# A two-layer hybrid backbone: RWKV block inverses from 16-blocks, alternating array halves, reordered filter positions, four column groups for the conditioning products

## The chip, the core and the metric

The kernel runs on one core of one Trainium2 chip as one program. The metric is the device time of one execution in microseconds (us). TensorE (PE) multiplies, VectorE (DVE), ScalarE (ACT) and GpSimd (POOL) do the elementwise work, SyncE (SP) issues nearly all DMAs. The profile shows weight loads of TensorE apart (PEld). Every instruction queue works in order; the program is built by a tile framework whose scheduler simulates the engines and writes out one fixed order for each of them.

## The reference, cut to what matters

Layer 0 runs retention and RWKV-7 side by side, layer 1 a Hyena long convolution and a neighbourhood attention. The change touches three parts.

RWKV-7 is a recurrence over 1280 tokens (256 of context, 1024 of latents), in both directions d, for 8 heads of width 64:

```python
def step(s, inp):
    r_t, w_t, k_t, v_t, kk_t, a_t = inp
    sa = jnp.einsum('bhvk,bhk->bhv', s, -kk_t)
    s = s * w_t[:, :, None, :] + sa[..., None] * (kk_t * a_t)[:, :, None, :] + v_t[..., None] * k_t[:, :, None, :]
    return s, jnp.einsum('bhvk,bhk->bhv', s, r_t)
```

The Hyena filters are a small network of the position, `h = sin(f2 * (sin(f1 * (z @ w1 + b1)) @ w2 + b2)) @ w3`, times a decay window, and go through an FFT of 2048 points. The conditioning (scale, shift and gate of both layers) is the product of silu(c) and silu(c_ctx), two vectors of 1024, with the weights `ada_w` of 1024 x 3072 per layer.

## The kernel before, in words

`phase_a` computes the conditioning of layer 0 (`ada_quarter`, eight blocks of 256 columns), the norm, the dense projections of layer 0 and the retention. `phase_b` is RWKV. `hyena_kernels` (filters and their spectra) begins in the last steps of `phase_b` and shares the time with `phase_c`, which projects layer 0 out. Then come the projections of layer 1, attention and the long convolutions.

**RWKV.** The tokens are cut into ten groups g of 128 tokens, each two chunks t of 64. Within a chunk the recurrence is a triangular system of 64 x 64 for each head and direction; per group there are 16 of them for each direction (2 chunks, 8 heads), direction 0 on partitions 0 to 63 and direction 1 on 64 to 127. Three stages are pipelined by `step(k)`: `recur` of group k-2, `merge` of group k-1, `stage1` of group k, with that priority.

- `stage1` calls `half` four times (direction d, head pair hp). `half` makes the low-rank products (`lora`, two weights, K of 64 rows), tanh, a running sum, exponentials, the scaled operands AR and BK and the transposes BT. Then the score products `sc` (K of 64 rows, one half of the partitions for each head h) are masked on DVE into Ga (the triangular matrices) and Gr. The tiles UV are cleared in one half by a memset on POOL, and the other half is loaded.
- `inverse` cuts each 64 x 64 triangle into two diagonal blocks of 32, writes them to DRAM (tensor la) and reads them back so that each partition holds one block (tile AL). It starts from an identity (RR, loaded from DRAM), runs 31 steps of a substitution with two DVE instructions each (`tm` and `RR`, L950 and L952), and sends the result back over DRAM (lt) into TT.
- `merge` joins the two 32-blocks by three products in a row (t11p, xp, t21p), each copied out of PSUM in two halves, by ACT and by DVE.
- `recur` does, for each chunk, the chain: `rp` from the state SP, `rp` from Ga, copies to RH, `up` with TT, copies to UV, `sp` into the state, two DVE instructions on S, copies to SP. The output products with Gr and the store of y follow.

UV and RH are cleared in the half that a product doesn't need, so that `rp` from Ga and `up` run over all 128 rows.

**Filling work.** `step` of `phase_b` also lets run the blocks of `RwkvOut` (FIN sets its buffers) and the rest of the conditioning, 32 blocks of 128 columns (`ada_gate`, `ada_cols`). In `ada_block` 8 products of 128 rows by 2 columns add up in one PSUM tile.

**Filters.** `hyena_kernels` takes for each channel tile, order and pair of positions the columns 2q+j, 2q+j+8, ... of `hid` as weights (stride 8), with K of 64 rows for each direction of the filter, and masks with the window on DVE.

## Time and profile before

| | us |
|---|---|
| three runs: 2420.06, 2421.17, 2431.53; median | 2421.17 |
| profiled execution, its own time | 2423.35 |
| its span, first to last instruction | 2421.6 |
| PE busy / DVE busy / ACT busy / POOL busy | 2233.8 / 1212.0 / 930.4 / 792.3 |
| mean granted TensorE clock, of full speed | 0.939 |

Busy time of PE is modelled from pipelined matmuls, so a busy PE isn't PE at its peak. A matmul in float32 appears as two instructions. Groups of instructions give the busy time of all, the mean time of one, and the idle time before them with what ended it.

### The profile page before, as it was taken

The page shows a single profiled execution, that of the slowest core. Times are in us where ns is not written, and L with a number is a line of the kernel's source. Part 1 is how long each engine was busy: PE and PEld are TensorE (multiplying, and loading weights), DVE is VectorE, ACT ScalarE, POOL GpSimd, SP SyncE. Part 2 cuts the span into 40 slices and gives each one's busy share as a digit, 9 for nine tenths or more (in the row PEclk, how much of TensorE's full clock was granted, in tenths as well). Part 3 has the DMA queues.
Part 4 walks back from the last instruction along what each step waited for, and adds up shares of the span by engine and source line. Part 5 has one row for each costly group of instructions (what it writes and reads, how often), then busy time and mean ns, then how long its engine had stood idle before and what let it go on. Part 6 is the DMA issues. An engine that isn't in the chain of part 4 may idle for free. (4 is left out here: it accounts for less than half of the span.)

```text
span 2421.6 us, 44498 instructions
## 1 busy us (share of the span) xinstructions
PE 2233.8 (92%) x16928; PEld 1880.8 (78%) x16928; DVE 1212.0 (50%) x3075; ACT 930.4 (38%) x1996; POOL 792.3 (33%) x1040
## 2 busy tenths in 40 slices
PE   7999999999989788899788999999989999989997
PEld 3778877777856677677676789889968888878987
DVE  6301222234348688777786645620036666634438
ACT  4321134445345353344335533322124444434432
POOL 2313626453556244333224433521120110010133
PEclk9999999999988687789979899999989999989999
DMA  7323334544276444455545334343166562275453
GB/s 246 94 75 105 118 113 128 151 122 135 91 212 183 113 122 129 108 136 143 132 121 169 118 122 141 118 147 109 57 178 162 148 168 83 65 226 153 133 175 122
DMA packets 398367, 325.16 MB, mean 134 GB/s; under 512 B 135038, under 2 KB 337928, under 8 KB 397898
## 3 DMA queue, kind: packets, MB, share of 16 engines
q1 hardware_dynamic: 398154, 322.32, 46.2%
q8 instruction: 134, 2.20, 0.4%
q14 instruction: 79, 0.65, 0.1%
HBM read 227.06 MB, written 95.17 MB: 133 GB/s over the span
## 5 line engine op out<-in xcount | busy, mean ns | idle before, releaser
L380 POOL TENSOR_TENSOR wlo<-wraw,whi 128x512 fp32r<-128x512 f32 (+1 forms) x60 | 82.5, 1393 | 359.9 <-ACT whi L379 304.9
L412 PE MATMUL dps<-n1hi,whi 128*128 128x512 f32 x448 | 186.7, 417 | 0.1
L412 PE MATMUL dps<-n1hi,wlo 128*128 128x512 f32 x448 | 176.2, 393 | 0.0
L412 PE MATMUL dps<-n1lo,whi 128*128 128x512 f32 x448 | 176.0, 393 | 0.0
L412 PE MATMUL dnp<-wlo,nhi 128*128 128x512 f32 x400 | 159.8, 401 | 2.9 <-POOL wlo L396 2.9
L412 PE MATMUL dnp<-whi,nlo 128*128 128x512 f32 x400 | 158.6, 398 | 0.0
L412 PE MATMUL dnp<-whi,nhi 128*128 128x512 f32 x400 | 154.0, 401 | 1.3 <-ACT whi L395 1.3
L396 POOL TENSOR_TENSOR wlo<-wraw,whi 128x512 fp32r<-128x512 f32 (+1 forms) x72 | 92.3, 1291 | 134.8 <-ACT whi L395 124.9
L412 PE MATMUL mmps<-nhi,whi 128*128 128x512 f32 (+1 forms) x336 | 123.7, 369 | 2.4 <-ACT vto L527 2.3
L321 PE MATMUL adaps<-aw,sc 128*2 128x128 f32 (+1 forms) x640 | 112.9, 333 | 9.9 <-DMA aw<-in_ada_w 9.4
L412 PE MATMUL mmps<-nlo,whi 128*128 128x512 f32 (+1 forms) x336 | 120.9, 362 | 0.0
L412 PE MATMUL mmps<-nhi,wlo 128*128 128x512 f32 (+1 forms) x336 | 119.6, 365 | 0.0
L950 DVE TENSOR_TENSOR tm<-RR,AL 128x126 f32<-128x126 f32 (+22 forms) x310 | 99.7, 322 | 19.3 <-DMA AL<-la 11.9
L1248 POOL TENSOR_TENSOR hn<-hn,xr 128x256 f32<-128x256 f32 x60 | 47.2, 791 | 173.4 <-DVE hn L1247 157.4
L952 DVE TENSOR_TENSOR RR<-RR,tm 128x126 f32<-128x126 f32 (+22 forms) x310 | 97.1, 313 | 6.2
L412 PEld LDWEIGHTS dps<-n1hi,wlo 128*128 128x128 f32 x448 | 84.5, 189 | 18.5
L321 PEld LDWEIGHTS adaps<-aw,sc 128*2 128x2 f32 x640 | 54.9, 94 | 53.7 <-issue 15.2
L412 PE MATMUL ops<-whi,clo 128*128 128x256 f32 x320 | 90.6, 290 | 5.4 <-DVE clo L1181 5.4
L412 PEld LDWEIGHTS dps<-n1hi,whi 128*128 128x128 f32 x448 | 85.5, 191 | 10.9 <-ACT whi L379 0.6
L412 PEld LDWEIGHTS dps<-n1lo,whi 128*128 128x128 f32 x448 | 85.2, 190 | 10.3
L412 PEld LDWEIGHTS dnp<-wlo,nhi 128*128 128x128 f32 x400 | 76.0, 190 | 22.1 <-POOL wlo L396 4.8
L412 PE MATMUL ops<-wlo,chi 128*128 128x256 f32 x320 | 91.7, 288 | 0.0
(400 smaller groups left out, 6235.6 us busy)
## 6 DMA issues: line engine op xcount, KB each, us to landing
aw<-in_ada_w SPq DMA_DIRECT2D x32, 512.0 KB
kkr<-kkr SPq DMA_DIRECT2D x40, 384.0 KB
wraw<-in_odd_w_in SPq DMA_DIRECT2D x56, 256.0 KB
wraw<-in_even_w_in SPq DMA_DIRECT2D x48, 256.0 KB
bi<-in_nab SPq DMA_DIRECT2D x64, 192.0 KB
aw<-in_ada_w SPq DMA_DIRECT2D x8, 1024.0 KB
spec<-KS SPq DMA_DIRECT2D x32, 256.0 KB
h<-hn SPq DMA_DIRECT2D x16, 512.0 KB
```

Source lines behind the costliest of these rows:

```text
L321: nc.tensor.matmul(ps[0:2, :n], self.sc[:, k, :], w[:, k, :], start=k == 0, stop=k == 7)
L380: (lo_eng or nc.gpsimd).tensor_tensor(lo[:, kk:kk + 4], raw, hi[:, kk:kk + 4].bitcast(F32), op=ALU.subtract)
L396: nc.gpsimd.tensor_tensor(lo[:, :n], raw[:, :n], hi[:, :n].bitcast(F32), op=ALU.subtract)
L412: nc.tensor.matmul(ps, a, b, start=start and n == 0, stop=stop and n == 3 * nk - 1)
L950: nc.vector.tensor_tensor(t3, RR[:, 0:n, q:q + 1].to_broadcast([P, n, w]), AL[:, q:q + 1, q + 1:32].to_broadcast([P, n, w]), op=ALU.mult)
L952: nc.vector.tensor_tensor(RR[:, 0:n, q + 1:32], RR[:, 0:n, q + 1:32], t3, op=ALU.add)
L1248: add.tensor_tensor(h[:, cs], h[:, cs], x[:, cs], op=ALU.add)
```

## The change

- The inverse takes 16 x 16 diagonal blocks: 15 steps with two DVE instructions each. The block result RR is also transposed on POOL (RT), and both go over DRAM into full 64 x 64 tiles dd and dt. Their off-diagonal parts are zeroed in DRAM once. The DRAM tensors have a row pitch in which the diagonal blocks of all matrices stand 1040 elements apart.
- N is Ga without its diagonal blocks, masked on POOL. `merge` forms HT from N and dt, and then three times X = dd + (HT times X). Each of the four products comes in two halves of eight matrices, through one PSUM tile each, and X is added on DVE.
- `rp` from Ga and `up` use only the 64 rows that hold data; RH has one half as many columns. The memsets of UV, RH and TT are gone.
- Low-rank products of both directions are issued in turn (`lora`), score products of both heads in turn, `sp` with the head as the inner loop. PSUM has three tiles `b1` in place of two and one for lora.
- y is stored by a DMA on ACT's queue. FIN is 5 in place of 6.
- `ada_block`: the vectors stand in 32 columns (30 of them zero), and product k goes to column group k % 4; the four sums are added by a later product with a selection matrix `sel`. The gate blocks need one product more for it.
- Filter positions stand in the order in which they are used, so the weights are 128 columns in a row; both directions are one product of 128 rows by 256 columns with a zero-padded w3, and one DVE instruction masks them.

```diff
-        self.sc = sc
+        self.sc = self.cp.tile([P, 8, 32], F32, name="scw")
+        nc.gpsimd.memset(self.sc, 0.0)
+        nc.vector.tensor_copy(self.sc[:, :, 0:2], sc)
...
         for k in range(8):
-            nc.tensor.matmul(ps[0:2, :n], self.sc[:, k, :], w[:, k, :], start=k == 0, stop=k == 7)
-        return ps[0:2, :n]
+            g = 32 * (k % 4)
+            nc.tensor.matmul(ps[g:g + 32, :n], self.sc[:, k, :], w[:, k, :], start=k < 4, stop=k > 3)
+        return ps[:, :n]
...
+        for j, w in enumerate((self.w2, self.a2)):
+            for q in range(2):
+                p = 2 * hp + q
+                for d in range(2):
+                    nc.tensor.matmul(pss[d][:, j, q, :], w[HALF[d], p * P:(p + 1) * P], wa[HALF[d], j, :], start=True, stop=True)
...
-                for h in range(2):
-                    ps = b1([P, 4, P], "sc")
-                    for p in range(4):
-                        u = (p % 2) * NS + t
-                        nc.tensor.matmul(ps[:, p, :], bks[d, p // 2][HALF[h], u, :], R["ar"][d, p // 2][HALF[h], u, :],
+                pss = [b1([P, 4, P], "sc") for _ in range(2)]
+                for p in range(4):
+                    u = (p % 2) * NS + t
+                    for h in range(2):
+                        nc.tensor.matmul(pss[h][:, p, :], bks[d, p // 2][HALF[h], u, :], R["ar"][d, p // 2][HALF[h], u, :],
...
-                nc.gpsimd.memset(UV[HALF[d]], 0.0)
...
+        for d in range(2):
+            nc.sync.dma_start(mats(LA, d), gu[d])
+        AL = pi.tile([P, 16, 16], F32, name="AL", tag="AL", bufs=2)
+        nc.sync.dma_start(AL, blocks(LA))
+        for d in range(2):
+            nc.gpsimd.tensor_tensor(N[HALF[d]], gu[d], s.k("off")[HALF[d], None, :].to_broadcast([C, 16, C]), op=ALU.mult)
+        RR = pi.tile([P, 16, 16], F32, name="RR", tag="RR", bufs=2)
+        nc.gpsimd.tensor_copy(RR, self.eye)
+        tm = pi.tile([P, 64], F32, name="tm", tag="tm", bufs=2)
+        for q in range(15):
+            n, w = q + 1, 15 - q
...
+        RT = pi.tile([P, 16, 16], F32, name="RT", tag="RT", bufs=2)
+        nc.gpsimd.tensor_copy(RT, RR.rearrange("p s t -> p t s"))
+        for L, src, n in ((LD, RR, "dd"), (LT, RT, "dt")):
+            nc.sync.dma_start(blocks(L), src)
+            T = R[n] = pl.tile([P, 16, C], F32, name=n, tag=n, bufs=1)
+            for d in range(2):
+                nc.sync.dma_start(T[HALF[d]], mats(L, d))
...
+        for j in range(4):
+            new = HT if j == 0 else TT
+            for b in (0, 8):
+                ps = self.pc.tile([P, 8, C], F32, name="mg", tag="mg")
+                for u in range(8):
+                    for d in range(2):
+                        lh, rh = (N, Dt) if j == 0 else (HT, X)
+                        nc.tensor.matmul(ps[HALF[d], u, :], lh[HALF[d], b + u, :], rh[HALF[d], b + u, :], start=True, stop=True)
+                bs = slice(b, b + 8)
+                if j == 0:
+                    nc.scalar.copy(new[:, bs], ps)
+                else:
+                    nc.vector.tensor_tensor(new[:, bs], ps, Dd[:, bs], op=ALU.add)
...
-            for h, p, d in each:
+            for p, d, h in itertools.product(range(4), range(2), range(2)):
                 nc.tensor.matmul(sp[HALF[h], p, d, :], R["bt"][d, p // 2][:, (p % 2) * NS + t, h * C:h * C + C], uh(d, t, p, h),
...
-                    for j in range(2):
-                        nc.tensor.matmul(ps[:, j, :], hid[r, 2 * q + j::8], w3[r], start=True, stop=True)
-                    nc.vector.tensor_tensor(HK[:, hf], ps, win[:, hf], op=ALU.mult)
+                ps = psp.tile([P, 2, 2, P], F32, name="hkps", tag="mm")
+                for j in range(2):
+                    n2 = 2 * q + j
+                    nc.tensor.matmul(ps[:, j].rearrange("p h c -> p (h c)"), hid[:, n2 * P:n2 * P + P],
+                                     w3.rearrange("p h c -> p (h c)"), start=True, stop=True)
+                nc.vector.tensor_tensor(HK, ps.rearrange("p j h c -> p h j c"), win, op=ALU.mult)
```

On PE, at the merge of one group in the middle of `phase_b`, before (t11p, xp and t21p are the merge, lora and up belong to `half` and `recur`):

```order
L973 MATMUL t11p<-cst,TT_6116 32x32 x32
L851 MATMUL lora<-wa,a_6097 128x128 x2
L851 MATMUL lora<-wa,w_6096 128x128 x2
L973 MATMUL xp<-TX,Ga 32x32 x32
L851 MATMUL lora<-wa,a_6097 128x128 x2
L973 MATMUL t21p<-TT_6116,TY 32x32 x32
L851 MATMUL lora<-wa,w_6096 128x128 x2
L996 MATMUL up<-RH,TT_6116 64x64 x16
```

The same place on PE after the change (mg are the halves of the four merge products, btp the transposes, sc the score products):

```order
L1005 MATMUL mg<-dt,N 64x64 x16
L912 MATMUL btp<-cst,BK 128x128 x4
L944 MATMUL sc<-AR,BK 128x128 x8
L1005 MATMUL mg<-dd,HTt 64x64 x16
L944 MATMUL sc<-AR,BK 128x128 x12
L1005 MATMUL mg<-dd,HTt 64x64 x16
L944 MATMUL sc<-AR,BK 128x128 x12
L1005 MATMUL mg<-TT,HTt 64x64 x16
L858 MATMUL lora<-wa,w_6102 128x128 x2
L858 MATMUL lora<-wa,a_6103 128x128 x2
```

Three bursts of 32 products have become eight of 16, with other products of `stage1` between most of them.

On SP, the DMAs of one inverse and what stands between them, before (la and AL out and in, lt and TT the way back; the others belong to `stage1` and the conditioning):

```order
L940 DMA la<-Ga 32x16x32 x2
L954 DMA lt<-RR 1024x1x32 x2
L943 DMA AL<-la 64x1024
L841 DMA kkr<-kkr 128x6x128 x2
L943 DMA AL<-la 64x1024
L958 DMA TT_6116<-lt 32x16x32 x4
L945 DMA RR<-in_eyel 128x512
```

And after it (ld, lt, dd and dt are the way back):

```order
L970 DMA la<-Ga 64x16x64 x2
L331 DMA aw<-in_ada_w 128x8x128
L972 DMA AL<-la 128x16x16
L331 DMA aw<-in_ada_w 128x8x128
L908 DMA prod<-km 128x256
L878 DMA kkr<-kkr 128x6x128
L908 DMA prod<-km 128x256
L878 DMA kkr<-kkr 128x6x128
L987 DMA ld<-RR 128x16x16
L987 DMA lt<-RT 128x16x16
L990 DMA dt<-lt 64x16x64 x2
```

The way back has two stores and four loads in place of two and four, and the load of the identity is gone.

## Rows read from the trace of the kernel before

**Rows 1.** Busy time of each engine in stretches of the span, with the granted clock and the DMA share: the stretch of RWKV as a whole, its start, and parts of it.
```profile
core 0: us, PE busy (x) PEld busy (x) DVE busy (x) ACT busy (x) POOL busy (x), PEclk, DMA share, GB/s
690.00:740.00 50.00, 47.65 (x355) 32.42 (x351) 27.99 (x62) 33.16 (x81) 29.76 (x45) 0.93 0.78 208
760.00:1250.00 490.00, 411.81 (x5783) 355.26 (x5783) 388.10 (x1096) 198.63 (x460) 167.38 (x271) 0.82 0.51 129
800.00:850.00 50.00, 38.14 (x574) 33.51 (x573) 31.65 (x94) 17.98 (x43) 10.40 (x15) 0.70 0.39 90
1210.00:1220.00 10.00, 5.64 (x136) 5.36 (x136) 9.37 (x27) 1.80 (x4) 2.44 (x2) 0.50 0.22 72
1250.00:1440.00 190.00, 180.03 (x1243) 149.79 (x1236) 112.96 (x256) 92.45 (x186) 86.95 (x93) 0.91 0.42 137
```

**Rows 2.** Timeline (start, duration, instruction): the first substitution step of the first and the last of the ten inverses, the last store of an inverse, and the last burst of the merge that follows.
```profile
745.43 0.19 DVE L950 TENSOR_TENSOR tm<-RR,AL 128x31 f32<-128x31 f32 x1 [1.22 <-DMA AL<-la]
...
1206.02 0.19 DVE L950 TENSOR_TENSOR tm<-RR,AL 128x31 f32<-128x31 f32 x1 [6.89 <-DMA AL<-la]
...
1236.19 1.26 SPq L954 DMA_DIRECT2D lt<-RR  x2
...
1259.80 0.94 PE L973 MATMUL t21p<-TT,TY 32*32 32x32 f32 x28
```

**Rows 3.** Groups of the whole span: the two instructions of a substitution step (count, busy us, mean ns).
```profile
L950 DVE TENSOR_TENSOR tm<-RR,AL 128x126 f32<-128x126 f32 (+22 forms) x310 | 99.7, 322 | 19.3 <-DMA AL<-la 11.9
...
L952 DVE TENSOR_TENSOR RR<-RR,tm 128x126 f32<-128x126 f32 (+22 forms) x310 | 97.1, 313 | 6.2
```

**Rows 4.** Groups by shape in 760 to 1250 us: substitution steps of the sizes that remain, a DVE copy of the merge, a DVE addition from PSUM, two POOL instructions.
```profile
L950 DVE TENSOR_TENSOR tm<-RR,AL 128x16 f32<-128x16 f32 x10 | 2.2, 217 | 0.2
L950 DVE TENSOR_TENSOR tm<-RR,AL 128x45 f32<-128x45 f32 x10 | 2.1, 214 | 0.2
L952 DVE TENSOR_TENSOR RR<-RR,tm 128x45 f32<-128x45 f32 x10 | 2.4, 244 | 0.3
L950 DVE TENSOR_TENSOR tm<-RR,AL 128x70 f32<-128x70 f32 x10 | 2.7, 274 | 0.3
L975 DVE COPY TX<-t11p 32x512 f32<-32x512 f32 x10 | 6.9, 689 | 0.7 <-ACT TX L975 0.4
L1004 DVE TENSOR_TENSOR S<-S,sp 128x512 f32<-128x512 f32 x18 | 12.3, 686 | 12.1 <-PE sp L1002 11.7
L880 POOL TENSOR_TENSOR km<-km,kkr 128x256 f32<-128x256 f32 x33 | 26.7, 808 | 1.0
L925 POOL MEMSET UV<- 64x512 f32 x32 | 16.6, 518 | 116.0 <-PE sp L1002 84.9 <-PE rp L1010 28.9 <-ACT BT L887 2.1
```

**Rows 5.** Groups by shape in 760 to 1250 us: the products of RWKV and of the conditioning on PE.
```profile
L915 PE MATMUL sc<-AR,BK 64*128 64x128 f32 x544 | 73.4, 306 | 4.1 <-DVE Gr L919 3.9
L321 PE MATMUL adaps<-aw,sc 128*2 128x128 f32 x363 | 56.5, 313 | 0.5 <-DVE mc L289 0.5
L1002 PE MATMUL sp<-UV,BT 128*64 128x64 f32 x576 | 38.9, 242 | 3.6 <-DVE UV L999 3.6
L851 PE MATMUL lora<-wa,w 64*128 64x128 f32 x124 | 27.8, 355 | 0.7 <-ACT tw L855 0.7
L851 PE MATMUL lora<-wa,a 64*128 64x128 f32 x124 | 27.3, 352 | 9.1 <-ACT tw L855 9.1
L996 PE MATMUL up<-RH,TT 128*64 128x64 f32 x576 | 26.5, 261 | 11.5 <-DVE RH L993 7.8 <-DVE TT L975 3.6
L990 PE MATMUL rp<-UV,Ga 128*64 128x64 f32 x576 | 22.4, 228 | 0.0
L973 PE MATMUL t11p<-cst,TT 128*32 128x32 f32 x640 | 15.4, 206 | 7.5 <-DMA TT<-lt 7.5
L973 PE MATMUL xp<-TX,Ga 32*32 32x32 f32 x602 | 15.1, 215 | 5.2 <-DVE TX L975 5.2
L973 PE MATMUL t21p<-TT,TY 32*32 32x32 f32 x576 | 15.0, 221 | 8.8 <-DVE TY L975 8.7
```

**Rows 6.** Timeline: one burst of t21p, whose products alternate between two row tiles of 32 and write to one PSUM tile.
```profile
1083.98 1.20 PE L973 MATMUL t21p<-TT,TY 32*32 32x32 f32 x64
```

**Rows 7.** DMA in 1053 to 1056 us, nearly all packets of 128 bytes: count and MB, and the queue's share of 16 engines.
```profile
DMA packets 2061, 0.57 MB, mean 191 GB/s; under 512 B 1981, under 2 KB 1981, under 8 KB 2061
...
q1 hardware_dynamic: 2061, 0.57, 101.9%
```

**Rows 8.** Groups by shape in 1250 to 1600 us: filter products with their weight loads, and the mask on DVE.
```profile
L1320 PE MATMUL hkps<-hw,hid 64*128 64x128 f32 x256 | 61.2, 434 | 6.3 <-ACT S L1362 2.9 <-DVE HK L1321 2.1 <-DMA hw<-in_hw 0.6
L1320 PEld LDWEIGHTS hkps<-hw,hid 64*128 64x128 f32 x256 | 52.4, 326 | 16.1 <-ACT S L1362 4.6 <-issue 3.8 <-DVE HK L1321 3.1
```

**Rows 9.** The start: conditioning products of 256 columns in 0 to 150 us, one burst of them in the timeline, the last burst, and the DMA share in 40 slices of 0 to 50 us.
```profile
L321 PE MATMUL adaps<-aw,sc 128*2 128x256 f32 x128 | 32.5, 412 | 8.8 <-DMA aw<-in_ada_w 8.8
...
13.77 3.62 PE L321 MATMUL adaps<-aw,sc 128*2 128x256 f32 x16
...
50.70 3.62 PE L321 MATMUL adaps<-aw,sc 128*2 128x256 f32 x16
...
DMA  0689999999999999999999999999999996000000
```

**Rows 10.** Group in 690 to 760 us: conditioning products of 128 columns. And the wait of t21p for DVE in 800 to 1200 us (us in total, times, longest).
```profile
L321 PE MATMUL adaps<-aw,sc 128*2 128x128 f32 x151 | 24.3, 312 | 0.6 <-DMA aw<-in_ada_w 0.6
...
PE t21p L973 <- DVE TY L975: 7.3, 4, 3.6
```

More of the change, by code (lines that the diff above doesn't have):

```diff
@@ L34 @@
 SD = (8,)
-FIN = 6
+FIN = 5
 def _col(a):
@@ L334, in ada_gate @@
                 nc.sync.dma_start(ab[j:j + 1, :], src)
-            nc.vector.tensor_tensor(rows, ps, ab, op=ALU.add)
-            nc.sync.dma_start(gd[:, c0:c0 + n], rows)
+            nc.vector.tensor_copy(rows, ps)
+            ps = psp.tile([P, 512], F32, name="adag", tag="mm")
+            nc.tensor.matmul(ps[0:2, :n], self.sel, rows, start=True, stop=True)
+            nc.vector.tensor_tensor(ab, ps[0:2, :n], ab, op=ALU.add)
+            nc.sync.dma_start(gd[:, c0:c0 + n], ab)
             yield
@@ L900, in stage1 @@
             nc.sync.dma_start(wa[HALF[d]], D["wa"][HALF[d], :, t0:t0 + P])
+        for hp in range(2):
+            tws = self.lora(g, hp, wa)
+            for d in range(2):
+                R["ar"][d, hp], bks[d, hp], R["bt"][d, hp] = self.half(g, d, hp, tws[d], PCt)
         for d in range(2):
             ca, cr = (0, 64) if d == 0 else (64, 0)
-            for hp in range(2):
-                R["ar"][d, hp], bks[d, hp], R["bt"][d, hp] = self.half(g, d, hp, wa, PCt)
             m = s.k("m0") if d == 0 else s.k("m1")
@@ L941, in inverse @@
[L941 to L948 removed]
+        s, D, pi, pl = self.s, self.D, self.pi, self.pl
@@ new lines, in inverse @@
+        nc, C = s.nc, self.C
+        gu = [R["ga"][d].rearrange("p h t q c -> p (h t q) c")[HALF[d]] for d in range(2)]
+        N = R["n"] = pl.tile([P, 16, C], F32, name="N", tag="N", bufs=1)
+        mats = lambda t, d: t[d].rearrange("(u s t) -> s u t", s=65, t=C)[0:C]
+        blocks = lambda t: t.rearrange("d (a n) -> (d a) n", n=1040)[:, :1024].rearrange("a (s t) -> a s t", t=C)[:, :, 0:16]
+        LA, LD, LT = (D[n][g % 2] for n in ("la", "ld", "lt"))
+        for d in range(2):
+            nc.sync.dma_start(mats(LA, d), gu[d])
@@ L956, in inverse @@
[L956 to L975 removed]
+                                    AL[:, q:q + 1, q + 1:16].to_broadcast([P, n, w]), op=ALU.mult)
@@ new lines, in inverse @@
+            nc.vector.tensor_tensor(RR[:, 0:n, q + 1:16], RR[:, 0:n, q + 1:16], t3, op=ALU.add)
+        RT = pi.tile([P, 16, 16], F32, name="RT", tag="RT", bufs=2)
[3 more added lines that the diff above has]
+            T = R[n] = pl.tile([P, 16, C], F32, name=n, tag=n, bufs=1)
+            for d in range(2):
+                nc.sync.dma_start(T[HALF[d]], mats(L, d))
@@ new lines, in merge @@
+    def merge(self, R):
+        nc, pl, C, N, Dd, Dt = self.s.nc, self.pl, self.C, R["n"], R["dd"], R["dt"]
+        HT = pl.tile([P, 16, C], F32, name="HTt", tag="HT", bufs=1)
+        TT = R["tt"] = pl.tile([P, 16, C], F32, name="TT", tag="TT", bufs=2)
+        X = Dd
+        for j in range(4):
[3 more added lines that the diff above has]
+                for u in range(8):
+                    for d in range(2):
+                        lh, rh = (N, Dt) if j == 0 else (HT, X)
[5 more added lines that the diff above has]
+                    nc.vector.tensor_tensor(new[:, bs], ps, Dd[:, bs], op=ALU.add)
+            if j > 0:
+                X = TT
```

134 lines of the change are left out of this document (52 added, 82 removed).

## Prediction

> **What bounds the kernel now.** I read the table of stretches first, then the groups by shape inside the RWKV stretch, the timeline at its start and end, and the waits. PE is nearly full before and after RWKV; in RWKV it isn't. From 760 to 1250 us PE is busy 411.8 of 490 us at a mean granted clock of 0.82, DVE 388.1, the DMA engines 51%, POOL and ACT far less [rows 1]. So neither PE (84%) nor DVE (79%) fills the stretch; each waits in order for the other, and both are loaded enough that a microsecond taken from either shortens part of the period. The period is (1206.02 - 745.43) / 9 = 51.2 us from one inverse to the next [rows 2], so the stretch holds 490 / 51.2 = 9.57 groups, each with 43.0 us of PE and 40.6 us of DVE. The last inverse has no next group to hide behind: 30 us pass from its first step to its store, and its merge ends at 1260 us [rows 2], in a stretch where PE has 5.64 of 10 us and DVE 9.37 [rows 1]. From 1250 to 1440 us PE is busy 180 of 190 us [rows 1]: there filter products cost nearly what they take.
>
> **DVE in RWKV.** Before, 620 instructions take 99.7 + 97.1 us [rows 3], 19.7 us a group. After, 30 remain, on 15 to 64 elements a partition. The sizes from 16 to 70 took 214 to 274 ns [rows 4]; I take 235, so 7.05 us, which is 12.6 less. Against it, the merge's three DVE copies (0.69 us each) become six additions from PSUM, near 0.686 each [rows 4]: 2.0 more. DVE net: 10.6 less of 40.6.
>
> **PE in RWKV.** Busy time divided by count gives the cost of one instruction in a stream [rows 5]; two stand for a product.
> - Column halves: `sp`, eight products in a row into the same half, costs 38.9 / 576 = 67 ns; `rp` from Ga, which alternates, 22.4 / 576 = 39 ns. `sp` goes to 39: 64 x 28 ns = 1.8 us less.
> - Row halves: sc costs 135 ns and lora 222 ns, both with K of 64 rows. No row of before shows two 64-row tiles in turn; the nearest is t21p, two row tiles of 32 in turn, 1.20 us for 64, some 19 ns each [rows 6]. Bounds: no gain, or half the time. I take half, being nearer that row: 64 x 67 ns = 4.3 us and 32 x 111 ns = 3.6 us less.
> - Conditioning: 56.5 / 363 = 156 ns, 38 a group. Four column tiles in turn reach at best a quarter, 39 ns, which is also what Ga's products cost: 4.4 us less, at worst none.
> - Merge: 45.5 us / 9.57 = 4.75 us before; after, 128 products, 256 instructions. At 39 ns 10.0 us, so 5.2 more; at xp's 25 ns 1.7 more, at the 67 ns of `sp` 12.4 more.
> - `up` and Ga with half the rows: the same number of products and columns, so nothing.
>
> Net 8.9 us less of 43.0.
>
> The Trainium skill (TensorEngine Tiling (Array Packing), Restrictions and Gotchas, PSUM pressure) says that different row tiles cannot access the same PSUM bank at the same time. Here merge and `up` have both direction halves in one tile; sc and lora have one each. The burst of t21p alternates row tiles into one tile at 19 ns an instruction [rows 6], which doesn't look like a rule in force. By the rule merge would cost what `sp` does; that case is the second rival.
>
> **The rest of RWKV.** POOL loses two memset pairs a group (4 x 0.52 us) and gains two masks of 64 x 1024, two copies of 128 x 256 (0.81 us for the nearest row, so some 1.6; the masks at the same rate 3.2 each) [rows 4]: 17.5 us a group becomes about 23, which 45 us hide. If not, the transposed copy RT, alone in the chain, costs 0.8. DMA: the shapes give 2048 + 128 + 128 + 2048 + 2048 = 6,400 packets an inverse before, 2048 + 2048 + 4096 + 4096 = 12,288 after, of 64 and 256 bytes. A small packet held an engine for 1.019 x 3 us x 16 / 2061 = 24 ns [rows 7]; 5,888 more are 8.8 us on each of 16 engines. With 0.51 x 51.2 = 26 us now, that is 35 of 45 us: transfers get later, they don't become the bound. An inverse has a whole period of slack in the pipeline, except the last. y on ACT's queue frees SP; ACT has 199 of 490 us busy [rows 1], so I cost it at nothing, as FIN, whose blocks are filling work.
>
> **The period.** With PE lighter by 8.9 and DVE by 10.6 the period falls by less than PE's share, since the merge now makes eight trips PE, PSUM, DVE in place of three, all through one PSUM bank, and each trip is a wait in PE's queue unless other products stand between. I take two thirds, 6 us (bounds 2 and 10). Nine periods: -54 us (-18 to -90).
>
> **The end of RWKV.** 62 instructions took 30.2 us, 0.487 each with what stands between; 30 take 14.6, so -15.6. Late in its place: RT 0.8, the way back with 4,096 packets more (6.1 us at 24 ns over 16 engines), AL with 1,920 more (2.9). Net -6 (0 to -16).
>
> **Filters.** 256 instructions at 61.2 us, 239 ns, are near what their strided weight load takes, 52.4 / 256 = 205 ns [rows 8]. After, 128 instructions of 256 columns; the conditioning products of 256 columns cost 32.5 / 128 = 254 ns [rows 9], so 32.5 us: 29 less. PE is 95% busy there, but has waits of its own, so I take -24 (-10 to -32).
>
> **Start.** A burst of 16 takes 3.62 us, the last begins at 50.7 us, while the DMA engines are full until slice 34 of 40, 42 us [rows 9]. Four column groups make bursts near 0.9 us, then the weights' arrival bounds: at most 9 us, less what the modulation between bursts keeps. I take -7 (0 to -9).
>
> **Conditioning from 690 to 760 us.** 151 instructions, 24.3 us [rows 10], 161 ns; at 39 ns 18.4 less; the 16 selection products of the gates add 32 x 156 ns = 5. PE is 95% busy there [rows 1], but DVE's inverse starts too: half of 13.4, -7 (0 to -13).
>
> **Sum.** -54 - 6 - 24 - 7 - 7 = -98 us. Against the profiled execution's 2423.35 that is 2325; it stands 2.2 us above the median of 2421.17, so 2323. All ends together: -160 (2261) and -28 (2393).
>
> **Rivals.**
> 1. The clock takes it back. A lighter PE is granted a lower clock: 0.50 where it is busy 5.64 of 10 us, 0.70 in 800 to 850 us where it is busy 38.1 of 50 [rows 1]. If RWKV falls from 0.82 to 0.70, 34.1 us of PE become 40, the period falls by only 2: -18 - 6 - 24 - 7 - 7 = -62, 2359. Against it: DVE falls too, and what PE did before those stretches was wait.
> 2. Row tiles in one bank go one after the other: merge at 67 ns, +12.5 in place of +5.2, `up` +1.4. PE's balance is then nil, the period falls by 1 for DVE's sake, the last merge is 8 us longer: -9 + 2 - 24 - 7 - 7 = -45, 2376. The t21p burst speaks against it.
> 3. Slower: the merge's eight trips through one bank stall PE. Where t21p waited for DVE it was 7.3 / 4 = 1.8 us a time [rows 10]. Eight such are 14.4 us a group, of which some 2.2 are there today (7.5 + 5.2 + 8.8 us over 9.57 groups, [rows 5]): +12.2, so the period grows by 6.2: +56, the end +6, the others -38: +24, 2445. It decides from (98 + 22) / 80 = 1.5 us a trip. For it: one bank, and DVE works in order. Against it: the new order puts transposes, score or low-rank products between nearly all bursts.
>
> **Chances.** Forecast 0.58 (its own range 2261 to 2393), rival 1 0.15, rival 2 0.14, rival 3 0.10, and 0.03 for mixtures near no change. The range for 8 in 10 is 2258 to 2400: it holds the first three and leaves out rival 3 and a larger gain. A change under 0.5% (12 us) is about what a measurement here cannot tell from none. Faster: 0.58 + 0.15 + 0.14 = 0.87. Same: 0.03 and 0.01 of rival 3, 0.04. Slower: 0.09.
>
> **What would show it.** Inverses some 45 us apart; substitution steps near 235 ns and 300 in all; sc near 67 ns and lora near 111 by busy time over count, with their heads and directions in turn; merge near 39 ns, and its waits for DVE under 0.5 us a trip; filter products near 254 ns, 128 of them; the first dense product some 7 us earlier. A granted clock near 0.7 in RWKV speaks for rival 1, merge at 67 ns for rival 2, long PE waits for TT and HT for rival 3. The forecast is wrong if the period stays above 49 us, or if the gain is found mainly outside RWKV.

## The result, and the profile after

| | before | after |
|---|---|---|
| median of the runs beside each other, us | 2426.35 (4 runs) | 2457.15 (4 runs, 2451.81 to 2460.11) |
| ratio of after to before, 95% interval | | 1.0113 (1.0075 to 1.0151) |
| profiled execution, its own time / span | 2423.35 / 2421.6 | 2455.93 / 2454.1 |
| last dense product of layer 0 begins, us | 676.80 | 663.99 |
| first step of the first / the last inverse | 745.43 / 1206.02 | 744.26 / 1266.69 |
| period of the inverses | 51.2 | 58.0 |
| output projection of layer 0 begins | 1398.6 | 1425.2 |

The change made the kernel 1.1% slower; 4.1% faster was forecast. Nothing of the forecast gain of 6 us a period came: the period grew by 6.9 us, and nine of them are 62 us. From the last inverse to the output projection the change takes 158.5 us in place of 192.6, so that 27 of them are left where the projection begins, and 31 at the end.

The table of stretches, columns as in [rows 1], first the end of the first phase, then RWKV, then the filters:

```profile
690.00:740.00 50.00, 36.10 (x311) 25.07 (x311) 23.84 (x56) 26.36 (x62) 31.95 (x42) 0.74 0.72 206
760.00:1290.00 530.00, 400.29 (x6112) 354.80 (x6104) 338.67 (x823) 185.76 (x449) 209.64 (x279) 0.78 0.55 126
1250.00:1440.00 190.00, 150.65 (x1583) 125.40 (x1584) 119.39 (x268) 84.53 (x174) 76.03 (x78) 0.89 0.47 139
```

The reader is to see that both loaded engines are less loaded than before: PE 76% in RWKV (84% in [rows 1]), DVE 64% (79%). A group takes longer although no engine is full: the stretch is bound by who waits for whom.

The timeline answering to [rows 2]: the first step of the first and of the last inverse, its two stores (ld is the way back of RR, lt that of the transposed block), the last burst of the last merge.

```profile
744.26 0.17 DVE L981 TENSOR_TENSOR tm<-RR,AL 128x15 f32<-128x15 f32 x1 [0.79 <-DMA AL<-la]
...
1266.69 0.83 DVE L981 TENSOR_TENSOR tm<-RR,AL 128x15 f32<-128x15 f32 x1 [0.60 <-DMA AL<-la]
...
1279.10 0.37 SPq L987 DMA_DIRECT2D ld<-RR  x1
1279.77 0.71 SPq L987 DMA_DIRECT2D lt<-RT  x1
...
1335.52 1.10 PE L1005 MATMUL mg<-TT,HTt 64*64 64x64 f32 x32
```

Groups of the whole span, answering to [rows 3] and [rows 4]: the substitution, the merge's additions, the mask of N.

```profile
L974 POOL TENSOR_TENSOR N<-Ga,cst 64x1024 f32<-64x1024 f32 x20 | 47.0, 2351 | 162.0 <-DVE Ga L947 143.1 <-PE mg L1005 18.8
L981 DVE TENSOR_TENSOR tm<-RR,AL 128x15 f32<-128x15 f32 (+4 forms) x150 | 45.0, 300 | 24.0 <-DMA AL<-la 20.4
L983 DVE TENSOR_TENSOR RR<-RR,tm 128x15 f32<-128x15 f32 (+4 forms) x150 | 42.6, 284 | 3.3
L1010 DVE TENSOR_TENSOR TT<-mg,dd 128x512 f32<-128x512 f32 x60 | 41.1, 685 | 7.2 <-PE mg L1005 6.3
```

Groups by shape in 760 to 1290 us, answering to [rows 5]:

```profile
L944 PE MATMUL sc<-AR,BK 64*128 64x128 f32 x576 | 58.9, 311 | 0.0
L1005 PE MATMUL mg<-TT,HTt 64*64 64x64 f32 x1152 | 53.6, 260 | 30.9 <-DVE TT L1010 30.8
...
L1024 PE MATMUL rp<-SP,AR 128*128 128x128 f32 x256 | 44.6, 341 | 18.0 <-ACT SP L1046 15.2 <-ACT Yg L1053 2.7
...
L1005 PE MATMUL mg<-dt,N 64*64 64x64 f32 x578 | 29.7, 255 | 10.9 <-DMA dt<-lt 10.8
L1040 PE MATMUL sp<-UV,BT 128*64 128x64 f32 x544 | 27.8, 263 | 4.5 <-DVE UV L1037 4.5
L1034 PE MATMUL up<-RH,TT 64*64 64x64 f32 x544 | 26.7, 255 | 23.7 <-DVE TT L1010 23.7
...
L1005 PE MATMUL mg<-dd,HTt 64*64 64x64 f32 x576 | 22.2, 231 | 7.1 <-ACT HTt L1008 5.0 <-DVE TT L1010 2.1
L335 PE MATMUL adaps<-aw,scw 128*32 128x128 f32 x328 | 19.9, 339 | 14.8 <-DVE adab L352 6.4 <-DVE fv L1108 6.1 <-DVE mc L302 1.7
L858 PE MATMUL lora<-wa,w 64*128 64x128 f32 x128 | 18.4, 347 | 0.0
L858 PE MATMUL lora<-wa,a 64*128 64x128 f32 x128 | 16.5, 314 | 0.0
```

Busy time over count: sc 102 ns (135 before), lora 34.9 / 256 = 136 (222), sp 51 (67), adaps 61 (156), merge 105.5 / 2306 = 46. So the cheaper products are there. The waits before mg and up for TT, 30.8 and 23.7 us, catch the eye; e2 and e12 below speak against their setting the period.

Where the low-rank products stand in PE's order, with the engines whose signal they wait for (one group of the change; lora makes the first pair of a group after the score products, the second pair after two btp):

```
2836 L944 MATMUL sc<-AR,BK 128x128 [waits PE_49]
2837 L858 MATMUL lora<-wa,w_6102 128x128 [waits DVE_49,PE_49] x2
...
2849 L912 MATMUL btp<-cst,BK 128x128 [waits Pool_49]
2850 L912 MATMUL btp<-cst,BK 128x128 x3
2851 L858 MATMUL lora<-wa,w_6102 128x128 [waits Activation_49] x2
```

Per group, 4 low-rank tiles, 4 of transposes and 8 of scores take turns in three tiles b1, in the order of the program. The first pair therefore waits for DVE, which masks the scores of the group before, the second for ACT, which copies the transposes of the first head pair out; those in turn wait for POOL's BK, the end of the chain that begins with the low-rank products. Before the change the low-rank tile was apart and waited only for ACT's own tanh. In the trace (1101.76 btp, 1102.35 lora; 1129.73 to 1131.44 sc, 1132.75 lora):

```profile
1101.76 0.66 PE L912 MATMUL btp<-cst,BK 128*128 128x128 f32 x4
1102.35 0.71 PE L858 MATMUL lora<-wa,w 64*128 64x128 f32 x8
...
1129.73 1.71 PE L944 MATMUL sc<-AR,BK 64*128 64x128 f32 x19
...
1132.75 0.71 PE L858 MATMUL lora<-wa,w 64*128 64x128 f32 x8
```

And POOL in between, which makes BK, stands still behind the mask of N, whose Ga comes with those scores:

```profile
1115.56 0.73 POOL L907 TENSOR_TENSOR km<-km,kkr 128x256 f32<-128x256 f32 x1
1128.14 2.35 POOL L974 TENSOR_TENSOR N<-Ga,cst 64x1024 f32<-64x1024 f32 x1 [11.85 <-DVE Ga L947]
1132.26 2.36 POOL L974 TENSOR_TENSOR N<-Ga,cst 64x1024 f32<-64x1024 f32 x1 [1.77 <-DVE Ga L947]
1137.31 0.72 POOL L905 TENSOR_TENSOR km<-km,kkr 128x256 f32<-128x256 f32 x1 [2.70 <-issue]
```

The Trainium skill (Perfetto Trace Analysis, Optimization Strategy) says that the same gap repeating on the engine that should be saturated can mean that there isn't enough SBUF or PSUM for the next tile. POOL isn't such an engine here, but its gap of 11.85 us repeats: 137.8 us in 14 such waits for Ga between 800 and 1260 us. The trace agrees so far as the gap changes with the tiles: in e6 below, which shares out the PSUM tiles in another way, the same mask waits 82.7 us in 7 waits between 800 and 1200 us, and not for Ga but for merge, which still reads the one buffer of N.

Last, the stores of the eight output blocks (RwkvOut) at the end of RWKV, before and after (count, ns min/median/max, start of the first and the last), and the stores of y in 1150 to 1380 us, before and after:

```profile
L1096 SPq DMA_DIRECT2D cat<-fo x8: 370/370/1276, 1205.4 to 1397.4; - x8
```
```profile
L1134 SPq DMA_DIRECT2D cat<-fo x8: 370/371/371, 1206.5 to 1424.0; - x8
```
```profile
L1018 SPq DMA_DIRECT2D y<-Yg x14: 446/462/547, 1160.9 to 1291.4; - x14
```
```profile
L1056 ACTq DMA_DIRECT2D y<-Yg x16: 452/452/478, 1159.9 to 1364.2; - x16
```

The projection begins at 1398.6 and 1425.2, 1.2 us behind the last block's store in both. I call this row of blocks the train. In the change it started on time and took 217 us in place of 192. By the program its blocks come in pairs, each behind the y of a later group, and the last y is stored at 1364.2 in place of 1291.4. The fifth block shows such a wait: its first load of y (fa) is issued at 1303.0, its second (fb) only at 1320.6, behind a y stored at 1317.4; before the change the two are issued at 1285.5 and 1286.0, and the y of that group was there by 1245.9.

### The profile page after: what moved, and what is told of

It reads as the page before. It is cut to its first block, busy times and chain, and to the rows that moved or that the text cites. A ratio compares the mean times of both kernels' runs of the same rounds, so it can differ in the third digit from the quotient of the medians.

```text
span 2454.1 us, 45258 instructions
## 1 busy us (share of the span) xinstructions
PE 2174.1 (89%) x17472; PEld 1851.5 (75%) x17472; DVE 1155.3 (47%) x2771; ACT 918.7 (37%) x1986; POOL 825.7 (34%) x1039
## 5 line engine op out<-in xcount | busy, mean ns | idle before, releaser
L397 POOL TENSOR_TENSOR wlo<-wraw,whi 128x512 fp32r<-128x512 f32 (+1 forms) x60 | 81.7, 1380 | 353.4 <-ACT whi L396 274.3
L413 POOL TENSOR_TENSOR wlo<-wraw,whi 128x512 fp32r<-128x512 f32 (+1 forms) x72 | 92.2, 1290 | 119.8 <-ACT whi L412 114.8
L974 POOL TENSOR_TENSOR N<-Ga,cst 64x1024 f32<-64x1024 f32 x20 | 47.0, 2351 | 162.0 <-DVE Ga L947 143.1
L429 PE MATMUL ops<-whi,chi 128*128 128x256 f32 x320 | 92.3, 291 | 0.0
L429 PEld LDWEIGHTS dnp<-whi,nlo 128*128 128x128 f32 x400 | 75.2, 188 | 17.5 <-issue 1.7
L1005 PE MATMUL mg<-TT,HTt 64*64 64x64 f32 x1280 | 59.0, 259 | 32.8 <-DVE TT L1010 32.7
```

The source lines that it names most:

```text
L397: (lo_eng or nc.gpsimd).tensor_tensor(lo[:, kk:kk + 4], raw, hi[:, kk:kk + 4].bitcast(F32), op=ALU.subtract)
L413: nc.gpsimd.tensor_tensor(lo[:, :n], raw[:, :n], hi[:, :n].bitcast(F32), op=ALU.subtract)
L429: nc.tensor.matmul(ps, a, b, start=start and n == 0, stop=stop and n == 3 * nk - 1)
L974: nc.gpsimd.tensor_tensor(N[HALF[d]], gu[d], s.k("off")[HALF[d], None, :].to_broadcast([C, 16, C]), op=ALU.mult)
L1005: nc.tensor.matmul(ps[HALF[d], u, :], lh[HALF[d], b + u, :], rh[HALF[d], b + u, :], start=True, stop=True)
```

## Experiments

All runs on one table; the ratio is to runs of the kernel before on the same chip. Period: (first step of the last inverse - that of the first) / 9. Train: stores of the first and the last of the eight blocks, us.

| run | median | ratio (95%) | period | train |
|---|---|---|---|---|
| after | 2457.2 | 1.0113 (1.0075 to 1.0151) | 58.0 | 1207 to 1424 |
| e1 outer parts only | 2405.5 | 0.9904 (0.9873 to 0.9935) | 53.5 | 1204 to 1390 |
| e2 32-blocks in the change | 2477.3 | 1.0192 (1.0150 to 1.0234) | 60.2 | 1223 to 1449 |
| e3 merge shares b1 | 2656.5 | 1.0924 (1.0875 to 1.0973) | 84.3 | 1334 to 1630 |
| e4 mask on DVE | 2442.4 | 1.0035 (1.0011 to 1.0060) | 56.5 | 1226 to 1434 |
| e5 own low-rank tile | 2480.1 | 1.0200 (1.0152 to 1.0247) | 52.9 | 1308 to 1489 |
| e6 own tile and order | 2437.1 | 1.0011 (0.9983 to 1.0038) | 50.0 | 1252 to 1432 |
| e7 before, shared | 2585.3 | 1.0628 (1.0588 to 1.0667) | 64.3 | 1268 to 1491 |
| e8 = e6, mask on DVE | 2410.6 | 0.9918 (0.9890 to 0.9946) | 51.0 | 1215 to 1407 |
| e9 order alone | 2480.6 | 1.0206 (1.0157 to 1.0254) | 56.5 | 1305 to 1485 |
| e10 = e8, sc in turn undone | 2421.3 | 0.9960 (0.9934 to 0.9986) | 50.0 | 1237 to 1416 |
| e11 = e1, recurrence changed | 2427.3 | 0.9985 (0.9957 to 1.0013) | 52.1 | 1260 to 1427 |
| e12 longer merge | 2506.5 | 1.0310 (1.0263 to 1.0357) | 59.0 | 1313 to 1497 |
| e13 = after, blocks first | 2471.3 | 1.0161 (1.0134 to 1.0187) | 60.2 | 1259 to 1452 |
| e14 = e6, blocks first | 2403.2 | 0.9876 (0.9850 to 0.9901) | 50.4 | 1212 to 1392 |
| e15 = e8, blocks first | 2417.2 | 0.9937 (0.9913 to 0.9960) | 49.8 | 1236 to 1416 |
| e16 = e1, blocks first | 2418.5 | 0.9933 (0.9905 to 0.9962) | 52.9 | 1203 to 1388 |
| e17 before, longer blocks | 2443.8 | 1.0041 (1.0021 to 1.0062) | 50.8 | 1202 to 1431 |
| e18 after, longer blocks | 2486.4 | 1.0228 (1.0211 to 1.0246) | 57.6 | 1270 to 1476 |

Each edit makes the scheduler write a new order of everything. A difference under 15 us between two kernels can come from another order as well as from the edit; I draw conclusions from larger ones, or from periods.

**e1, outer parts only.** The class `Rwkv` of before with its tensors la and lt, all else of the change:

```diff
-FIN = 5
+FIN = 6
...
-    def lora(self, g, hp, wa):
...
+    def half(self, g, d, hp, wa, PCt):
```

> RWKV is left as it was; only the conditioning products on four column groups and the filter part are taken from the change. Theory (the whole loss sits in RWKV, the other parts gain): about 2426 - 13 (end of the first phase) - 15 (filters) = 2398, period between inverses 51 us. Rival (the outer parts cost something inside RWKV, since the conditioning blocks run there with more copies on DVE): 2420 or more, with a period above 52 us.

Measured 2405.5, ratio 0.9904: 26 us faster than the runs beside it. The outer parts gain and RWKV loses it. But the period is 53.5, not 51.2:

```profile
739.00:1220.00 481.00, 402.59 (x5341) 353.66 (x5340) 365.76 (x1023) 195.04 (x456) 173.31 (x286) 0.73 0.50 127
```

PE's busy time is 402.59 / 481 x 53.5 = 44.8 us a group at a clock of 0.73, 43.0 at 0.82 before, although conditioning products cost 69 ns in place of 156. Inside RWKV their gain isn't to be seen: the score products, which e1 leaves as they were, went from 135 to 82.3 / 543 = 152 ns (760 to 1200 us).

**e2, the inverse and merge of before in the change.**

```diff
-        for q in range(15):
+        for q in range(31):
...
-        for j in range(4):
+        for nm, rows, dst, op in (
+                ("t11p", e, lambda d: TX[e[d]], lambda d, u: (TT[:, u, 0:32], ident[:, e[d]])),
...
```

> The change with the inverse and the merge of before (32-blocks, 31 steps, three products); the alternating halves, the half-width products, no clearing, the new order of the low-rank and score products, the filters and the conditioning stay. Theory (the 16-block inverse with its long merge sets the period): the period falls from 58 to 47 to 51 us, 2350 to 2395. Rival (the new order of the low-rank and score products delays the triangular matrices): the period stays at 55 or more, 2430 to 2460.

Measured 2477.3, period 60.2. My theory of that time, that the long merge sets the period, fell: without the new inverse the change is 20 us slower still. The first step and the last:

```profile
745.35 0.19 DVE L978 TENSOR_TENSOR tm<-RR,AL 128x31 f32<-128x31 f32 x1 [4.35 <-DMA AL<-la]
...
1287.49 0.19 DVE L978 TENSOR_TENSOR tm<-RR,AL 128x31 f32<-128x31 f32 x1 [1.16 <-DMA AL<-la]
```

**e3, a second bank for merge, out of the b1 rotation.**

```diff
-                ps = self.pc.tile([P, 8, C], F32, name="mg", tag="mg")
+                if b and not last:
+                    ps = self.b1([P, 8, C], "mg")
+                else:
+                    ps = self.pc.tile([P, 8, C], F32, name="mg", tag="mg")
```

> The second half of each merge product goes to another PSUM tile (one of the three b1 tiles) for all groups but the last, so that a burst need not wait until DVE has emptied the tile of the burst before. Rival 3 of the prediction (one PSUM bank): the waits of merge for DVE fall from 31 us to under 10 and the time by 20 to 40 us, 2415 to 2435. Theory (the chain of dependent bursts, not the bank): within 10 us of 2457.

Measured 2656.5, period 84.3: neither. The question of the bank wasn't answered, since the tile came from b1; but it showed how much hangs on that rotation.

**e4, the mask of N on DVE.**

```diff
-            nc.gpsimd.tensor_tensor(N[HALF[d]], gu[d], s.k("off")[HALF[d], None, :].to_broadcast([C, 16, C]), op=ALU.mult)
+            nc.vector.tensor_tensor(N[HALF[d]], gu[d], s.k("off")[HALF[d], None, :].to_broadcast([C, 16, C]), op=ALU.mult)
```

> The mask that makes N is issued on DVE in place of POOL, so POOL no longer stands 138 us in the stretch behind the score products. Theory that POOL's order sets the period (the next group's scaled operands wait behind N): the time falls by 30 us or more, to 2425 or less. Theory (merge chain): the time stays within 10 us of 2457, since the merge is no earlier.

Measured 2442.4: 15 us less than the change, period 56.5. Between the two expectations, and no more than the 15 us above: POOL's order may cost something, the bulk lies elsewhere.

**e5 and e6, the low-rank tile apart, then the order too.** In e5 the products of one direction follow those of the other:

```diff
-        return self.pb.tile(shape, F32, name=name, tag="b1", bufs=3)
+        return self.pb.tile(shape, F32, name=name, tag="b1", bufs=2)
...
+        ps = self.pb.tile([P, 2, 2, P], F32, name="lora", tag="lo", bufs=1)
```

e6 on top of it:

```diff
-        for hp in range(2):
-            for d in range(2):
-                R["ar"][d, hp], bks[d, hp], R["bt"][d, hp] = self.half(g, d, hp, wa, PCt)
         for d in range(2):
+            for hp in range(2):
+                R["ar"][d, hp], bks[d, hp], R["bt"][d, hp] = self.half(g, d, hp, wa, PCt)
```

> The low-rank products go back to a PSUM tile of their own (one, as before), for one direction after the other; b1 has two tiles again; the order of the four calls of half, all else of the change and its inverse stay. Theory (shared rotation: the low-rank products of the next half wait until the transposes of this one are out, since they take turns in the same three tiles, so the halves no longer overlap): the period falls from 58 to 50 or less, 2345 to 2390. Rival (the order: score products only after all four halves): the period stays within 2 us of 58, 2440 to 2460.

> As the run before, and the score products of a direction again follow its two halves, as before the change; the score products of both heads still alternate. Shared rotation: no better than the run before by more than 10 us. Order: 20 us or more better than it.

The period falls from 58.0 to 52.9 and to 50.0; the times are 2480 and 2437. So the theory was right on the period, in the larger part, and wrong on the time: e5 has a period 5 us shorter than the change and is 23 us slower. Its first inverse begins 20 us later (764.7), its last still 25 us earlier (1241.2), but its train starts 101 us later. Of the 43 us from e5 to e6 (20 or more were expected of the order) nine periods of 2.9 us are 26; the train starts 55 us earlier. The first step of the first and the last inverse of e6:

```profile
743.90 0.15 DVE L970 TENSOR_TENSOR tm<-RR,AL 128x15 f32<-128x15 f32 x1
...
1194.05 1.76 DVE L970 TENSOR_TENSOR tm<-RR,AL 128x15 f32<-128x15 f32 x1 [2.36 <-DMA AL<-la]
```

The stretch of e6, and from its timeline what stands still in the train (POOL, then PE and DVE):

```profile
744.00:1194.00 450.00, 369.13 (x5711) 326.15 (x5711) 297.20 (x734) 187.15 (x441) 201.33 (x276) 0.82 0.62 140
```
```profile
1175.14 1.26 POOL L1114 TENSOR_TENSOR fa<-fa,lnwb 128x512 f32<-128x512 f32 x1 [4.29 <-DVE fa L1111]
```
```profile
1239.92 1.05 PE L1096 MATMUL bon<-rkh,fp 128*128 128x2 f32 x8
1241.01 0.69 DVE L1097 TENSOR_TENSOR fv<-fv,bon 128x512 f32<-128x512 f32 x1 [0.28 <-PE bon L1096]
1241.78 1.27 POOL L1098 TENSOR_TENSOR fv<-fv,lnwb 128x512 f32<-128x512 f32 x1 [31.18 <-DVE fv L1097]
```

The first block's sum fa is ready at 1176.4, its product bon, a filler in PE's order, comes at 1239.9.

**e7, the shared rotation in the kernel before.**

```diff
-        ps = self.pb.tile([P, 2, 2, P], F32, name="lora", tag="lo", bufs=1)
+        ps = self.b1([P, 2, 2, P], "lora")
...
-        return self.pb.tile(shape, F32, name=name, tag="b1", bufs=2)
+        return self.pb.tile(shape, F32, name=name, tag="b1", bufs=3)
```

> The kernel before with one edit: its low-rank tile takes its turn in the b1 rotation, of three tiles in place of two (as many banks in all). Shared rotation: it slows by 30 to 80 us, to 2455 to 2505, period 55 to 60. Rival (only the paired products or the order cost): within 10 us of 2426.

Measured 2585.3, 152 us slower (30 to 80 expected) with as many banks and no other edit; period 64.3:

```profile
767.66 0.19 DVE L950 TENSOR_TENSOR tm<-RR,AL 128x31 f32<-128x31 f32 x1 [2.88 <-DMA AL<-la]
...
1346.38 0.19 DVE L950 TENSOR_TENSOR tm<-RR,AL 128x31 f32<-128x31 f32 x1 [2.62 <-DMA AL<-la]
```

The longest waits of the stretch are those of the chain from the low-rank products to the transposes:

```profile
POOL AR L870 <- ACT Pt L864: 195.8, 28, 14.4
ACT BT L887 <- PE btp L885: 64.8, 24, 7.2
...
PE btp L885 <- POOL BK L879: 60.5, 18, 9.0
```

This is the plainest of the runs: the shared rotation by itself costs 13 us a period, more than the change loses. The change has it in a milder form; that this comes from its asking for low-rank tiles in pairs is likely, but no run shows it.

**e8, e6 with the edit of e4 on top** (the mask on DVE).

> Own low-rank tile and order as before, and the mask of N on DVE. Theory (once the halves overlap, POOL's wait behind the score products is what holds them next, as the 15 us of the run with the mask on DVE alone suggest): 5 to 20 us below the same kernel with the mask on POOL. Rival (the merge chain holds it): no difference over 5 us.

Measured 2410.6, 26 us less than e6, more than expected; the period is no shorter (51.0), the train starts 38 us earlier. The expected mechanism isn't what gained.

**e9, order alone.** Low-rank products of all four halves first, d the outer loop, three shared tiles.

```diff
-        for hp in range(2):
-            tws = self.lora(g, hp, wa)
-            for d in range(2):
-                R["ar"][d, hp], bks[d, hp], R["bt"][d, hp] = self.half(g, d, hp, tws[d], PCt)
+        tws = [self.lora(g, hp, wa) for hp in range(2)]
         for d in range(2):
...
+            for hp in range(2):
+                R["ar"][d, hp], bks[d, hp], R["bt"][d, hp] = self.half(g, d, hp, tws[hp][d], PCt)
```

> The change with one thing of its first stage undone in another way: the three shared tiles stay, but the low-rank products of all four halves come first, and the score products of a direction follow its two halves. The low-rank products of the second head pair no longer stand behind the transposes of the first. (Tiles for their results: 5 in place of 3; operands kkr: 2 in place of 3, as before the change.) Theory (low-rank products behind transposes and late score products are the loss, not the number of tiles): period 50 to 54, 2400 to 2440. Rival (any sharing of the tiles costs as much as in the kernel before with a shared rotation): 2480 or more, period 60 or more.

Measured 2480.6, period 56.5: the theory's 50 to 54 was missed. Even asked for early, low-rank tiles in the shared rotation hold the period; order alone is worth 1.5 us.

**e10, e8 with the score products of one head after the other; e11, e1 with the recurrence of the change** (half-width products, no clearing, sp in turn, y on ACT's queue). First e10's core, then two of e11's lines:

```diff
-                pss = [b1([P, 4, P], "sc") for _ in range(2)]
+                for h in range(2):
+                    ps = b1([P, 4, P], "sc")
```
```diff
-                nc.gpsimd.memset(UV[HALF[d]], 0.0)
...
-                nc.sync.dma_start(o[t if d == 0 else 1 - t], Y[r])
+                nc.scalar.dma_start(o[t if d == 0 else 1 - t], Y[r])
```

> The fastest version so far with the change's inverse (own low-rank tile, order as before, mask on DVE), its score products again one head after the other. Theory (pairs take both b1 tiles at once, so that products and masks take turns): 5 to 20 us faster, 2390 to 2405. Rival (alternating halves save PE time that counts): slower by 5 to 15 us.

> The outer parts of the change (run e1) and of RWKV only the recurrence: half-width products, no clearing of UV and RH, alternating state products, y stored from ACT's queue. Inverse, merge and first stage as before. Theory (what is alone on the loop gains, and POOL no longer waits 95 us for sp): 2375 to 2398. Rival (the stores on ACT's queue or half-width products cost): 2406 or more.

Both theories missed, both rivals came: e10 is 11 us slower than e8, which is within the 15 us above, e11 22 us slower than e1. In e10 sc costs 67.3 / 512 = 131 ns in 760 to 1200 us, in e8 59.9 / 512 = 117; the period is the same within 1 us, but the train starts 22 us later. In e11 the period is 1.4 us shorter than in e1, and its train starts 56 us later.

**e12, a merge of twelve bursts in place of eight.**

```diff
-        for j in range(4):
+        for j in range(6):
```

> The change with two more products in merge, in the same chain (the result stays the same, since the series has ended): 12 bursts in place of 8, 64 matmuls more a group. If the merge chain stands on the path that sets the period, each burst costs 3 to 4 us: 4 x 3.5 x 9 = +126, 2560 to 2600. If it has slack, only PE's busy time grows, 128 x 46 ns = 6 us a group in an engine that is three quarters busy: 0 to +40, 2457 to 2500.

Measured 2506.5, between; but the period is 59.0 against 58.0:

```profile
745.68 0.17 DVE L981 TENSOR_TENSOR tm<-RR,AL 128x15 f32<-128x15 f32 x1 [0.39 <-DMA AL<-la]
...
1276.25 0.17 DVE L981 TENSOR_TENSOR tm<-RR,AL 128x15 f32<-128x15 f32 x1 [3.06 <-DMA AL<-la]
```

Four more trips through the bank cost under 1 us a period of 58 us; what they would cost at a period of 50 us wasn't run. The 49 us arise behind the last inverse: the train starts 106 us later.

**e13 to e16, output blocks at RWKV's own priority**, and nothing else:

```diff
-                    next(blocks, None)
+                    with tc.high_priority(offset=1000000):
+                        next(blocks, None)
...
-        for _ in blocks:
+        while True:
+            with tc.high_priority(offset=1000000):
+                if next(blocks, 0) == 0:
+                    break
```

> The change, with the output blocks (RwkvOut) at RWKV's own priority. Train theory: here the train started on time (its first block is stored at 1207 us, before the change at 1205) and then waits for late y, so little can be won: 2440 to 2460. Rival (filling work at a low priority is what is late everywhere): 2420 or less.

> Own low-rank tile and order as before (period 50.0; 2437 us), with the output blocks at RWKV's own priority. Train theory: the first block no longer stands still from 1175 to 1240 us, the train starts 40 to 60 us earlier, and the end comes 20 to 45 us earlier: 2390 to 2417. Rival (the end is set by the filters or by the load of PE): within 8 us of 2437.

> The same with the mask on DVE (2411 us), where the train stood from 1174 to 1196 only. Train theory: 10 to 20 us earlier, 2390 to 2402. Rival: no change.

> The old RWKV with the outer parts of the change (2406 us), where the train started as soon as its y was there. Train theory: within 8 us of 2406. Rival: faster by 15 us or more.

e14 came as expected: 34 us less than e6, 2403.2, faster than the kernel before (0.9876) and with e1 the fastest that was run. Its period is e6's, its train (same view as above) starts 40 us earlier:

```profile
L1123 SPq DMA_DIRECT2D cat<-fo x8: 370/370/384, 1212.2 to 1391.7; - x8
```

The three others missed by 5 to 15 us, on the slow side, and are 7 to 14 us slower than the same kernels without the edit. The priority doesn't always bring the train forward: in e13 it started 53 us later than in the change, in e15 21 us later than in e8, and the times follow the train. In e16 the train is as in e1 and the time 13 us longer, without a cause that I can show.

**e17 and e18, longer output blocks:** eight Newton steps of the reciprocal root in place of four.

```diff
-        r = s.rsqrt(pl, x, "fr", 8)
+        r = s.rsqrt(pl, x, "fr", 8, its=8)
```

> The kernel before, with eight Newton steps in place of four in each output block (12 DVE instructions of 8 columns more, 4 to 7 us a block; the result stays the same). Train theory: 7 or 8 blocks pass it on, the projection starts 28 to 50 us later, and the time is 2455 to 2480. Rival (RWKV's period or the filters set the end): 8 x 3 us of DVE work hidden, within 10 us of 2431.

> The same in the change, whose train waits for late y between its blocks. Train theory: a part of the added time falls into these waits: +10 to +35, 2467 to 2492. Rival: within 8 us of 2457; if the train bounds it throughout, +40 or more.

The train of e17, and the products of the projection up to 1440 us:

```profile
L1096 SPq DMA_DIRECT2D cat<-fo x8: 370/371/770, 1202.2 to 1430.8; - x8
```
```profile
L412 PE MATMUL ops<-whi,chi x15: 279/282/684, 1430.9 to 1439.6; 128*128 128x256 f32 x15
```

In e17 the train takes 229 us in place of 192, and the projection begins 32 us later, as the train theory has it; but the time grows by 10 us only, at the edge of what the rival expected. PE filled the wait with filter products that it otherwise has left behind the train: from 1398 to 1431 us, before the projection begins, it is busy 28.4 of 33 us. So in the kernel before, the train gates the projection, and that PE's filter work is nearly as long, so that both bound the end, fits the 10 us. In the change (e18) the time grows by 29 us, as expected in number, but that is luck: its train takes 206 us in place of 217 and starts 64 us later, so the run doesn't show what longer blocks cost there.

## Why the prediction was wrong, point by point

**The step that failed: "each waits in order for the other, and both are loaded enough that a microsecond taken from either shortens part of the period."** In e6 and e14 the low-rank tile and the order are mended, DVE has 297.2 / 450 x 50.0 = 33 us a group in place of 40.6, PE 41 in place of 43.0, and the period is 50.0 to 50.4 in place of 51.2. So 7.6 us less on DVE and 2 us less on PE bought about 1 us. Two shares near 80% didn't mean that the engines bound the stretch. In the sum it is the term of -54 us for nine periods (bounds -18 to -90): +62 us were measured in the change, and with tile and order mended (e6) some -10.

**What was left out: PSUM tiles and the order of the first stage.** I listed "PSUM has three tiles b1 in place of two and one for lora" and gave it no cost. It is the main cause of the longer period: giving the low-rank products their own tile takes 5.1 of the 6.9 us (e5), the order of the halves 2.9 more (e6), and the same sharing costs 13 us a period in the kernel before (e7). e5 and e9 undo more than one thing, so the split between tile and order is an estimate, good to 1 or 2 us at best.

**The other term at nothing: "I cost it at nothing, as FIN, whose blocks are filling work."** The projection begins 1.2 us behind the last of these blocks, and e6 and e14, which are the same in RWKV and have nearly the same period, end 34 us apart with trains that end 40 us apart. That FIN is 5 isn't what makes the train long: e14, with five buffers, has it in 180 us, the kernel before, with six, in 192.

**PE's terms.** Predicted sc 67, lora 111, sp and adaps 39, merge 39 ns; measured 102, 136, 51, 61, 46. By count: -2.1, -2.8, -1.0, -3.6, and +7.0 for merge (256 x 46 ns = 11.8 for 4.75), together -2.5 in place of -8.9. Part of it is that products which weren't touched got dearer too: rp from AR went from 38.7 / 288 = 134 to 174 ns, rp from Gr from 47.4 / 576 = 82 to 88, at a mean clock of 0.78 in place of 0.82. Busy time is 400.29 / 530 x 58.0 = 43.8 us a group, no less than before.

**DVE's terms.** Steps cost 87.6 / 300 = 292 ns, not 235: 8.8 us a group for 7.05. The additions cost 4.1 us as predicted. A group has 338.67 / 530 x 58.0 = 37.1 us of DVE, 3.5 less than before in place of 10.6; the longer group also holds more filling work.

**"An inverse has a whole period of slack."** It held for the merge of the change, at its longer period (e12: +1 us for four trips).

**The end of RWKV.** The last substitution takes 12.4 us from first step to store, 17.8 less ([rows 2]; 15.6 predicted). But from there merge runs to 1336.6, 57 us behind the store, since its eight bursts alternate with the recurrence; before, it was 25. From first step to last burst it is 69.9 us for 54.7: 15 more in place of 6 less.

**Filters.** Near the prediction, 35.1 / 128 = 274 ns (254 predicted), 26 us less PE time against 29:

```profile
L1357 PE MATMUL hkps<-hw,hid 128*128 128x256 f32 x128 | 35.1, 399 | 4.5 <-ACT S L1400 2.9 <-ACT d2r L1413 0.7 <-DVE HK L1359 0.5
```

What I didn't see is that the projection behind them waits for the train. PE at 180 of 190 us [rows 1] looked like a bound, and e17 shows that it is one beside another.

**Start and conditioning.** Bursts of 16 take 1.94, later 1.07 us in place of 3.62, and the last dense product begins 12.8 us earlier, more than the 7 us (0 to 9) put down for the start. But at the first inverse, where the 7 us for the conditioning from 690 us on should have come on top, only 1.2 us are left: from 690 to 740 us PE is busy 36.1 us in place of 47.65, so a full PE isn't what held RWKV's first groups. In e1, with the old RWKV, 6 us were kept.

**The rivals.** Rival 3 came near in time (2445) but not in cause: its trips would have to cost 1.5 us each; PE waited 30.8 us for TT over nine groups of eight, 0.4 us a trip, or 0.75 with the 23.7 us of up. Its sign, long waits for TT, so came in part; but e12 added four trips for 1 us a period, and e2, with the old merge, has no shorter period. Rival 2: merge at 46 ns, not 67. Rival 1: the clock fell from 0.82 to 0.78, not to 0.70, while the period grew; in e1 it fell to 0.73, the score products got dearer and the conditioning's gain was lost, which is this rival in small, though PE is busy 84% of the stretch in both and what brought the clock down isn't shown.

**What stays open.** What sets 50 us once the tiles are apart, with PE at 82% and DVE at 66%, wasn't found; POOL's wait for N isn't it, since with the mask on DVE (e8) the period is 51.0. A merge with a second bank of its own wasn't run. Nor was it found why the scheduler starts the train where it does; by the table that goes with much of the scatter between the versions; e16, whose train is that of e1, can't be explained by it.

## What to carry to other kernels

A pool's rotation is an order: when tiles of different kinds take turns in it, the first step of a chain waits for the last step of the chain before, and merging two pools of one and two tiles into one of three can cost much without a bank being lost (e7). Before pricing an edit by busy shares, look for what follows strictly one after the other, here the chain of a half and the train of output blocks, and ask which of them the stretch's last instruction waits for. Filling work that something later waits for isn't filling work: e14 gained 34 us by priority alone. But the same edit made three other versions 7 to 14 us slower, so it has to be measured each time.
